# The second half of a feed-forward, with weight pairs that move on one by one

## The chip, the cores and the metric

One core of a Trainium2 chip runs the whole program. The metric is the device time of one execution in microseconds; for the kernel before it is the median of three runs. The profile is of one execution, with times counted from the first instruction.

## The reference

One layer of a hybrid encoder for 2048 tokens (16 learned ones are put in front, and dropped at the end), model width 1024, feed-forward width 2816, all float32. The change lies in the last step:

```python
f = causal_dwconv(rms_norm(h, norm_ffn_pre[l]) @ ffn_up[l], ffn_conv[l])
gate, val = jnp.split(f, 2, axis=-1)
f = (jax.nn.gelu(gate, approximate=True) * val) @ ffn_down[l]
h = h + rms_norm(f, norm_ffn_post[l])
```

The stages before it (an input projection with three groups of heads, attention among them, and an output projection) aren't touched.

## The kernel before

Matrix products in float32 are made of three passes over split operands: each operand is kept as a high and a low part (`split`: ScalarE copies the high part, then VectorE or GpSimd subtracts it from the source to get the low one), and `mm3` multiplies high by high, high by low and low by high.

The **up stage** (`ffn_up`) walks over 3 groups of tokens times 22 blocks of 128 columns, a unit each. A unit makes seven products by a scheme that saves one of eight (Strassen's in Winograd's form: sums and differences of operands go in, and sums of products come out). Its products use three PSUM banks, and two sets of three alternate between units. Then come a convolution of three taps (`conv`: one ScalarE instruction, L1723, and two on VectorE, L1725), a GELU on ScalarE, the gate times value on GpSimd (L1731), and a store to the scratch tensor `ff`. `between` runs at the start of each unit and weaves other work in: normalising the next tokens, sums of the down weights, and, in one unit of the last group, the first weights of the down stage.

The **down stage** (`Down`) multiplies `ff` by `ffn_down`. The 2816 rows are taken as ten pairs of 256 rows and a rest of 256. The tokens are taken as eight blocks of 256. A weight pair is seven operands of 128 x 512, high and low, of which four are sums that lie ready in the scratch tensor `ds`; `down_operands` loads each into a raw buffer (L1814, 256 KB) and splits it (L1594 on ScalarE, L1595 on VectorE for five and on GpSimd for two). For each visit of a token block to a weight pair, `side` loads the activations `u` (L1831), makes four sums on GpSimd (L1838 to L1841) and splits seven blocks into `fo`, of which two buffers exist. Then come seven products of three passes each.

Operand slots are 35, enough for five pairs: nine on the space of the up stage's activations (`kept`, tile name `qd`) and 26 in a ring of three pools (`dw`). So the stage runs in two halves:

```python
for pair in range(pairs):
    steps.first(pair, ks[0], weights)
...
for pair in range(pairs):
    steps.second(pair, ks[1], weights, last)
```

`first` visits each token block with pairs 0 to 4 and stores partial sums to the scratch tensor `part`. `second` visits each with pairs 5 to 9 and with the rest, adds `part` on GpSimd (L1883), and ends with `add_normed`: squares summed on ScalarE, a root, a scaling by root and gain (L1522) and an addition to the residual (L1523), and the store. Between the two halves all 35 operands are replaced.

A visit accumulates in seven PSUM banks (eight with the rest) of a pool of eight, which lies where the up stage's banks were. The order of the instructions on each engine is made ahead by a scheduler that works by program order and its own timeline; each engine then runs its queue in that order. All the loads and stores in question are issued on SyncE's queue.

## Time and profile before

| | |
|---|---|
| median of three runs | 3072.59 us (3067.38, 3072.59, 3078.05) |
| profiled execution | span 3071.8 us; its own time isn't told apart from the runs |
| mean granted TensorE clock | 0.969 |
| TensorE matmul busy | 2921.6 us (95%) |
| VectorE, ScalarE, GpSimd busy | 2054.8, 1482.3, 1358.8 us |
| up stage on TensorE | 1678.5 to 2597.2 us |
| down stage on TensorE | 2597.3 to 3060.3 us |

PE is TensorE, DVE VectorE, ACT ScalarE, POOL GpSimd, SP SyncE. A row names a line of the kernel, an engine, an operation, and the tile it writes and those it reads. In a row of a window stand the stretch, its length, and for each engine the busy time with the number of instructions, then the granted TensorE clock (1.00 is full), the mean busy share of the DMA engines, and GB/s. In a row of a wait stand who waited, what ended the wait, and the sum, the number and the longest of them in us. In a row of a tile stand the least, middle and greatest duration in ns, and the first and last start. In a timeline stand start and duration in us, and in brackets the idle time before it and who ended it. Matmuls overlap: one of 512 columns is shown with 390 ns, and the next starts 230 ns after it.

### The profile page before, as it was taken

The page shows a single profiled execution, that of the slowest core. Times are in us where ns is not written, and L with a number is a line of the kernel's source. Part 1 is how long each engine was busy: PE and PEld are TensorE (multiplying, and loading weights), DVE is VectorE, ACT ScalarE, POOL GpSimd, SP SyncE. Part 2 cuts the span into 40 slices and gives each one's busy share as a digit, 9 for nine tenths or more (in the row PEclk, how much of TensorE's full clock was granted, in tenths as well). Part 3 has the DMA queues.
Part 4 walks back from the last instruction along what each step waited for, and adds up shares of the span by engine and source line. Part 5 has one row for each costly group of instructions (what it writes and reads, how often), then busy time and mean ns, then how long its engine had stood idle before and what let it go on. Part 6 is the DMA issues. An engine that isn't in the chain of part 4 may idle for free. (4 is left out here: it accounts for less than half of the span.)

```text
span 3071.8 us, 52793 instructions
## 1 busy us (share of the span) xinstructions
PE 2921.6 (95%) x18694; PEld 2495.2 (81%) x18694; DVE 2054.8 (67%) x3934; ACT 1482.3 (48%) x2853; POOL 1358.8 (44%) x1589
## 2 busy tenths in 40 slices
PE   6999999999989999999989899999999999999998
PEld 6998898888876654665558899999999998787876
DVE  5268645656667785556635788888778786547766
ACT  4245332443336553555534656666566665324333
POOL 1001121122114555667842457445655444547765
PEclk9998999999988898999999999999999999999999
DMA  6776578466654346535245555566777765435444
GB/s 211 244 237 207 161 244 287 156 211 204 196 153 94 88 104 199 133 99 122 62 129 173 168 182 180 169 201 208 214 215 216 219 189 171 161 104 171 149 160 144
DMA packets 467818, 532.58 MB, mean 173 GB/s; under 512 B 85488, under 2 KB 355514, under 8 KB 466000
## 3 DMA queue, kind: packets, MB, share of 16 engines
q1 hardware_dynamic: 467168, 528.81, 56.5%
q8 instruction: 147, 2.41, 0.3%
q14 instruction: 119, 0.97, 0.1%
q0 software_dynamic: 384, 0.39, 0.0%
HBM read 369.11 MB, written 159.95 MB: 172 GB/s over the span
## 5 line engine op out<-in xcount | busy, mean ns | idle before, releaser
L172 PE MATMUL psu<-xo,uw 128*128 128x344 f32 x1848 | 589.9, 323 | 16.7 <-ACT xo L1594 6.9
L173 PE MATMUL psu<-xo,uw 128*128 128x344 f32 x1848 | 592.6, 321 | 0.0
L174 PE MATMUL psu<-xo,uw 128*128 128x344 f32 x1848 | 582.9, 320 | 0.0
L172 PE MATMUL psp<-xh,wh 128*128 128x384 f32 (+2 forms) x1152 | 383.6, 333 | 4.1 <-ACT wh L166 2.4
L174 PE MATMUL psp<-xh,wl 128*128 128x384 f32 (+2 forms) x1152 | 380.7, 331 | 3.5 <-DMA wl<-scr_wk 3.5
L173 PE MATMUL psp<-xl,wh 128*128 128x384 f32 (+2 forms) x1152 | 380.5, 330 | 0.0
L172 PEld LDWEIGHTS psu<-xo,uw 128*128 128x128 f32 x1848 | 346.9, 188 | 20.3 <-ACT xo L1594 7.1
L1595 DVE TENSOR_TENSOR uw<-uq,uw 128x512 fp32r<-128x512 f32 x341 | 316.2, 933 | 70.3 <-ACT uw L1594 63.7
L173 PEld LDWEIGHTS psu<-xo,uw 128*128 128x128 f32 x1848 | 347.9, 188 | 0.3 <-DVE xo L1595 0.3
L174 PEld LDWEIGHTS psu<-xo,uw 128*128 128x128 f32 x1848 | 346.5, 188 | 0.0
L1594 ACT ACTIVATE uw<-uq 128x512 fp32r<-128x512 f32 x462 | 287.9, 627 | 110.1 <-PE psu L174 48.7
L686 ACT ACTIVATE p<-sc,bias 128x512 f32<-128x512 f32 (+4 forms) x352 | 195.8, 590 | 178.5 <-PE sc L682 146.3
L1725 DVE SCALAR_TENSOR_TENSOR uy<-psu,ffn_cols,uy 128x342 f32<-128x342 f32 (+1 forms) x396 | 223.9, 567 | 60.7 <-ACT uy L1723 59.1
L559 DVE TENSOR_REDUCE mc<-mx 128x1 f32<-128x512 f32 (+6 forms) x352 | 190.3, 565 | 100.9 <-PE mx L554 75.8
L1731 POOL TENSOR_TENSOR uy<-uy,uy 128x342 f32<-128x342 f32 (+1 forms) x132 | 140.6, 1065 | 253.2 <-DVE uy L1725 77.4
L725 POOL TENSOR_TENSOR acc<-acc,p 128x512 f32<-128x512 f32 (+3 forms) x208 | 221.8, 1068 | 60.3 <-ACT p L686 23.9
L1595 POOL TENSOR_TENSOR uw<-uq,uw 128x512 fp32r<-128x512 f32 x121 | 177.9, 1470 | 125.0 <-ACT uw L1594 92.7
L174 PEld LDWEIGHTS psp<-xh,wl 128*128 128x128 f32 x1152 | 222.1, 193 | 13.0 <-issue 6.1
L172 PEld LDWEIGHTS psp<-xh,wh 128*128 128x128 f32 x1152 | 222.1, 193 | 10.7 <-issue 4.0
L173 PEld LDWEIGHTS psp<-xl,wh 128*128 128x128 f32 x1152 | 222.1, 193 | 7.6 <-issue 5.5
L1595 DVE TENSOR_TENSOR fo<-u,fo 128x896 fp32r<-128x896 f32 x88 | 112.6, 1279 | 121.3 <-ACT fo L1594 121.3
L1594 ACT ACTIVATE fo<-u 128x896 fp32r<-128x896 f32 x88 | 81.1, 922 | 206.3 <-POOL u L1841 106.8
(465 smaller groups left out, 6470.4 us busy)
## 6 DMA issues: line engine op xcount, KB each, us to landing
uq<-scr_us SPq DMA_DIRECT2D x220, 256.0 KB
uq<-in_ffn_up_dram SPq DMA_DIRECT2D x209, 256.0 KB
wl<-scr_wk SPq DMA_DIRECT2D x48, 512.0 KB
wh<-scr_wk SPq DMA_DIRECT2D x48, 512.0 KB
u<-scr_ff SPq DMA_DIRECT2D x88, 256.0 KB
scr_ff<-uy SPq DMA_DIRECT2D x110, 171.0 KB
raw<-in_w_in_dram SPq DMA_DIRECT2D x24, 512.0 KB
scr_wk<-wh SPq DMA_DIRECT2D x24, 512.0 KB
```

What stands on the lines that cost most here:

```text
L172: nc.tensor.matmul(out, ah, bh, start=first, stop=False, skip_group_check=more)
L173: nc.tensor.matmul(out, ah, bl, start=False, stop=False, skip_group_check=more)
L174: nc.tensor.matmul(out, al, bh, start=False, stop=last, skip_group_check=more)
L559: self.reduced = nc.vector.tensor_reduce(mc[:rows, i, ci : ci + 1], ps[:rows, : e - a], axis=AX.X, op=ALU.max)
L686: last = nc.scalar.activation(p[:rows, :w], ps[:rows, :w], AF.Exp, bias=bias[:rows, j : j + 1])
L725: eng.tensor_tensor(a, ps_[0][0][:rows, c0:n] if start and i == 1 else a, p[:rows, : n - c0], op=ALU.add)
L1594: core.nc.scalar.activation(hi, src, AF.Copy)
L1595: (eng or core.nc.vector).tensor_tensor(lo, src, hi, op=ALU.subtract)
L1725: stt(y[:, :n], src[:, i : n + i], cw[:, 44 * i + cc : 44 * i + cc + 1], y[:, :n], op0=ALU.mult, op1=ALU.add)
L1731: core.pooled = nc.gpsimd.tensor_tensor(v[:, :n], g[:, :n], v[:, :n], op=ALU.mult)
```

## The change

- **Moving pairs.** A visit still takes five weight pairs, but they move on: in the first half, block p starts at pair 5p // 8, so that blocks 0 to 7 start at pairs 0, 0, 1, 1, 2, 3, 3, 4. In the second half each block takes the five that it hasn't had, by the same rule starting at 5 and counted around from ten to zero. Pairs 0 to 3 are therefore prepared a second time, as 10 to 13: 14 preparations in place of 10. Slots are reused in a fixed ring of 35.
- **Four more kept slots.** The pools of the normalised tokens and their gain (`np`, `gf`) are opened outside the up stage, and their four tiles become operand slots there; the ring's second pool has four fewer. So 13 operands, not 7, are prepared during the last group of the up stage: pair 0 at unit 13 and six of pair 1 at unit 17.
- **Held splits.** The remaining splits of pairs 0 to 3 are queued behind the up stage's last convolution instruction on ScalarE and on VectorE (an order of issue on that engine alone).
- **Rest weights.** They are loaded in the seventh visit of the first half, queued behind that visit's last ScalarE copy of `la` and last store.
- **Banks read by copies.** In the last unit of the up stage the sums of products p3 and p2 are written to the tiles `u2` and `ga` rather than to their bank, and p4 is copied to a tile by ScalarE, and the convolutions read these.
- **`add_scaled`** takes the place of `add_normed` in the down stage: the gain is multiplied in before the root is ready, and the root comes in with the addition.

```diff
+def add_scaled(core, pool, halves, gain, x, junk):
+
+    nc = core.nc
+    v = pool.tile([P, 8], F32, tag="rs2", name=core.n("rs2"))
+    sums = v[:, 4:5], v[:, 5:6]
+    for y, acc in zip(halves, sums):
+        nc.scalar.activation(junk, y, AF.Square, accum_out=acc)
+    for c, y in enumerate(halves):
+        nc.vector.tensor_tensor(y, y, gain[:, 512 * c : 512 * c + 512], op=ALU.mult)
+    r1 = rstd_root(core, v, sums, D)
+    for c, y in enumerate(halves):
+        xc = x[:, 512 * c : 512 * c + 512]
+        nc.vector.scalar_tensor_tensor(xc, y, r1, xc, op0=ALU.mult, op1=ALU.add)
...
-DOWN_KEPT = 9
-
-DOWN_SLOTS = 5, 13, 8
-DOWN_TURNS = (2, 3), (0, 5), (1, 13), (2, 5)
-DOWN_FROM = 14
+DOWN_KEPT, DOWN_NORM = 9, 3
+
+DOWN_SLOTS = 5, 9, 8
+DOWN_TURNS = (2, 3), (0, 5), (1, 9), (2, 5)
+DOWN_FROM = 13, 17
+DOWN_HELD = 4
+DOWN_REST = 6
...
             elif name == "p3":
-                tt(ps, ps, u2, op=ALU.add)
-                gb = conv(ps, 0, j, n[1])
+                sum_ = ps if more else u2
+                tt(sum_, ps, u2, op=ALU.add)
+                gb = conv(sum_, 0, j, n[1])
...
             else:
-                va = conv(ps, 1, j, n[0])
+                src = ps
+                if not more:
+                    src = s("ga")
+                    nc.scalar.activation(src, ps, AF.Copy)
+                va = conv(src, 1, j, n[0])
                 ending(ga, va, j, b0[0], n[0])
...
+def down_visits(pairs):
+
+    for half in range(2):
+        for pair in range(pairs):
+            first = DOWN_CUT * pair // pairs + DOWN_CUT * half
+            yield half, pair, range(first, first + DOWN_CUT)
...
         for k in ks:
-            side, w = self.side(k, pair), weights(k)
+            side, w = self.side(k % DOWN_PAIRS, pair), weights(k)
...
-            add_normed(core, self.spool, halves, P, self.gain, hx, [junk] * 2)
+            add_scaled(core, self.spool, halves, self.gain, hx, junk)
...
+        def slot():
+            down.append(down.pop(0))
+            home = down[-1]
+            return home.tile([P, 2, 512], F32R, tag="dw", name=core.n("dw")) if hasattr(home, "tile") else home
...
                 down.extend(kept[:, i] for i in range(DOWN_KEPT))
+                for pl, tag in [(np_, "nt_x")] * DOWN_NORM + [(gf, "g_fpre")]:
+                    down.append(pl.tile([P, 2, 512], F32R, tag=tag, name=core.n("kd"))[:])
             elif sup == SUPERS:
-                if j == DOWN_FROM:
+                if j in DOWN_FROM:
                     raw = lambda: tmp.tile([P, 512], F32, tag="uq", name=core.n("raw"))[:]
-                    ws.append(down_operands(core, raw, lambda: down.pop(0), a["ffn_down"], scr, 0))
+                    k = DOWN_FROM.index(j)
+                    some = range(min(len(DOWN_PRODUCTS), len(down) - len(DOWN_PRODUCTS) * k))
+                    ws[k] = down_operands(core, raw, slot, a["ffn_down"], scr, k, some)
...
+        down[:0] = [dws[i] for i, n in DOWN_TURNS for _ in range(n)]
...
+        ended = core.taken.ins, core.conved.ins
+
+        def weights(c):
+            have = ws.setdefault(c, [])
+            if len(have) < len(DOWN_PRODUCTS):
+                raw = lambda: dwr.tile([P, 512], F32, tag="dq", name=core.n("raw"))[:]
+                with ExitStack() as behind:
+                    for ins in ended if c < DOWN_HELD else ():
+                        behind.enter_context(tc.issue_after(ins))
+                    some = range(len(have), len(DOWN_PRODUCTS))
+                    have += down_operands(core, raw, slot, a["ffn_down"], scr, c % DOWN_PAIRS, some)
+            return have
...
+        for half, pair, ks in down_visits(pairs):
+            if half == 0:
+                steps.first(pair, ks, weights)
...
+                if pair == DOWN_REST:
+                    with tc.issue_after(core.copied.ins), tc.issue_after(core.stored.ins):
+                        for i in range(2):
+                            rest.append(dwn.tile([P, 2, D], F32R, tag=f"r{i}", name=core.n("dwn")))
+                            at = P * (2 * DOWN_PAIRS + i)
+                            load_parts(core, (dpo, "hx", None), a["ffn_down"][at : at + P, :], rest[i][:, 0], rest[i][:, 1])
+            else:
+                steps.second(pair, ks, weights, last)
```

`core.taken` and `core.conved` are the up stage's last ScalarE and VectorE convolution instructions, `core.copied` and `core.stored` the down stage's last copy of `la` and last store of `part` at that point.

67 lines of the change are left out of this document (24 added, 43 removed).

## The prediction

> **What bounds the kernel now.** I read the first and second part of the page first, then the second half of the feed-forward (from about 2597 us to the end) in windows, then the waits of TensorE alone there, and the timeline around the two places where those waits lie.
>
> ```profile
> span 3071.8 us, 52793 instructions
> ...
> PE 2921.6 (95%) x18694; PEld 2495.2 (81%) x18694; DVE 2054.8 (67%) x3934; ACT 1482.3 (48%) x2853; POOL 1358.8 (44%) x1589
> ```
>
> TensorE is the bound over the whole span, so only its idle time can be won back. How many matmuls this stage has is told by the rows of its accumulator tiles, one form of three:
>
> ```profile
> L172 PE MATMUL psd<-dw,fo x416: 388/392/632, 2612.9 to 3054.4; 128*128 128x512 f32 x139
> ...
> L172 PE MATMUL psd<-qd,fo x144: 390/395/765, 2597.3 to 3035.4; 128*128 128x512 f32 x144
> ...
> L172 PE MATMUL psd<-dwn,fo x64: 388/394/394, 2841.7 to 3059.9; 128*128 128x512 f32 x64
> ...
> L174 PE MATMUL psd<-dwn,fo x64: 388/392/394, 2842.8 to 3060.3; 128*128 128x512 f32 x64
> ```
>
> 416 + 144 + 64 = 624, times three passes: 1872 matmuls. By the code these are eight visits of 5 x 7 x 3 = 105 and eight of 105 + 24 = 129. In windows of the stage (first visit; visits two to seven; the last of the first half and the first of the second; the other seven; the tail):
>
> ```profile
> core 0: us, PE busy (x) PEld busy (x) DVE busy (x) ACT busy (x) POOL busy (x), PEclk, DMA share, GB/s
> 2597.00:2637.00 40.00, 31.54 (x109) 23.68 (x108) 26.44 (x30) 22.03 (x35) 22.10 (x26) 0.79 0.66 227
> 2637.00:2782.00 145.00, 145.00 (x631) 118.41 (x631) 68.85 (x81) 38.06 (x48) 75.06 (x121) 1.00 0.32 107
> 2782.00:2847.00 65.00, 58.22 (x235) 45.52 (x235) 54.39 (x55) 32.30 (x52) 49.79 (x52) 0.95 0.56 183
> 2847.00:3061.00 214.00, 211.21 (x905) 168.59 (x903) 149.88 (x192) 72.51 (x136) 142.17 (x163) 1.00 0.47 155
> 3061.00:3071.80 10.80, 0.00 (x0) 0.00 (x0) 6.36 (x14) 2.17 (x8) 0.54 (x1) 0.66 0.41 146
> ```
>
> Visits two to seven are the undisturbed pace: 145.00 / 6 = 24.17 us, or 0.2302 us a matmul, so a visit of 129 should take 29.70. Cut at their first matmuls, the two visits of the third window are
>
> ```profile
> 2782.04:2810.66 28.62, 24.78 (x107) 19.40 (x105) 24.82 (x25) 15.91 (x26) 23.34 (x22) 1.00 0.65 211
> 2810.66:2847.17 36.51, 33.57 (x130) 26.25 (x131) 29.69 (x31) 16.39 (x27) 26.62 (x31) 0.91 0.49 161
> ```
>
> The lost time is then: first visit 39.7 (2597.3 to 2637.0) - 24.17 = 15.6; the change of halves 28.62 + 36.51 - 24.17 - 29.70 = 11.3; the last seven 214.0 - 7 x 29.70 = 6.1, or 0.87 each. In all 33.0 us, 1.1% of the span: this is the most that the stage can give. What TensorE waited for, in the first window, the third, and the fourth:
>
> ```profile
> PE psd L172 <- DVE uy L1725: 3.0, 1, 3.0
> PE psd L172 <- ACT uy L1727: 2.9, 1, 2.9
> PE psd L173 <- DVE dw L1595: 2.1, 1, 2.1
> PE psd L172 <- ACT dw L1594: 0.4, 1, 0.4
> ```
> ```profile
> PE psd L172 <- ACT fo L1594: 3.9, 2, 3.7
> PE psd L174 <- DVE fo L1595: 2.7, 2, 2.3
> ```
> ```profile
> PE psd L172 <- ACT fo L1594: 2.3, 5, 0.6
> ```
>
> So two causes, not one. At the start TensorE waits for banks that the convolution of the last up unit still reads (uy), then for weights (dw). At the change of halves it never waits for a weight: it waits for the activation operand `fo`, whose sums and splits (`side`) queue behind a burst of 35 weight operands on ScalarE, VectorE and GpSimd.
>
> **The change, part by part.** *Banks and the held splits.* The timeline of VectorE and of TensorE at the start:
>
> ```profile
> 2595.88 2.44 DVE L1595 TENSOR_TENSOR dw<-raw,dw 128x512 fp32r<-128x512 f32 x3 [0.19 <-ACT dw L1594]
> ...
> 2600.02 1.04 DVE L1725 SCALAR_TENSOR_TENSOR uy<-psu,ffn_cols,uy 128x342 f32<-128x342 f32 x2
> ...
> 2604.98 0.57 DVE L1725 SCALAR_TENSOR_TENSOR uy<-psu,ffn_cols,uy 128x342 f32<-128x342 f32 x1
> ```
> ```profile
> 2605.69 0.76 PE L172 MATMUL psd<-qd,fo 128*128 128x512 f32 x1 [2.87 <-ACT uy L1727]
> 2606.26 0.63 PE L173 MATMUL psd<-qd,fo 128*128 128x512 f32 x1
> 2606.68 0.63 PE L174 MATMUL psd<-qd,fo 128*128 128x512 f32 x1
> ```
>
> Weight splits sit between the last convolutions, the last of which ends at 2605.6, and the bank goes free only then. After the change the sums land in `u2` and `ga`, and product p4 is copied out by one ACT instruction, so the last bank is free about one copy after the last up matmul; the splits of pairs 1 to 3 on ScalarE and VectorE queue behind the last convolution, which should then end near 2600.5 instead. The copy adds one ACT instruction (nearest row 0.63 us, below) on a chain that nobody in this visit waits for. Both bank waits go: 3.0 + 2.9. With them goes most of the slow pace behind them: matmuls at 2606 take 0.63 us against a usual 0.39, and about a dozen start 0.43 apart, about 3 us in all. That is 9 of the 15.6.
>
> *What is late next: the weights.* Thirteen operands are ready instead of seven, so the visit needs 22 more. Eight fit the raw buffers and lie loaded; then the hold keeps them from being split until about 2599 (ScalarE) and 2600.5 (VectorE). The other 14 loads wait behind that in SP's queue, and with them the loads of `u`, which ScalarE and GpSimd need for `fo`. 14 + 5 transfers of 128 x 512 x 4 bytes are 5.0 MB, at the 227 GB/s of the first window 22 us: from 2600.5 to 2622.5, and the split of the last comes behind. An unbroken visit ends at 2621.5. Prices of one operand, and of one `fo` split:
>
> ```profile
> L1594 ACT ACTIVATE dw<-raw x52: 612/629/635, 2594.7 to 2828.6; 128x512 fp32r<-128x512 f32 x52
> L1595 DVE TENSOR_TENSOR dw<-raw,dw x36: 678/944/1774, 2595.9 to 2831.9; 128x512 fp32r<-128x512 f32 x36
> L1595 POOL TENSOR_TENSOR dw<-raw,dw x16: 1267/1533/1824, 2599.7 to 2828.7; 128x512 fp32r<-128x512 f32 x16
> ...
> L1595 DVE TENSOR_TENSOR fo<-u,fo x88: 691/1230/2187, 2586.7 to 3051.1; 128x896 fp32r<-128x896 f32 x80, 128x512 fp32r<-128x512 f32 x8
> ```
>
> VectorE: 16 of the 22 at 0.944 is 15.1, and four `fo` splits at 1.23 another 5: 20 us from 2600.5, to 2620.6, just in time if nothing collides. I take a loss of 5 us (3 late, 2 of slow pace) where 15.6 was; bounds 0 and 15.6.
>
> *The rest weights* (two loads of 512 KB, two splits on ScalarE and on VectorE) leave the first visit, where the first is issued at
>
> ```profile
> 2602.58 0.42 SPq L165 DMA_DIRECT2D raw<-in_ffn_down_dram  x1
> ```
>
> for the seventh, behind a copy and a store of it. This is 1 MB, some 4.6 us of transfers at that rate, off the tightest place; it is in the 5 us above. In the seventh visit I cost it at nothing: ScalarE works 38.06 of 145 us there. Without that cover it would be two operands of double size, under 4 us.
>
> *Six more operands in the up stage.* Work of this kind falls into
>
> ```profile
> 2480.00:2520.00 40.00, 40.00 (x255) 40.00 (x254) 34.01 (x55) 26.55 (x55) 18.39 (x16) 1.00 0.72 207
> 2520.00:2560.00 40.00, 40.00 (x255) 40.00 (x254) 29.91 (x49) 24.36 (x50) 13.14 (x14) 1.00 0.58 165
> ```
>
> TensorE is full in both. Six operands add at most 4 x 0.944 to VectorE, 6 x 0.629 to ScalarE, 2 x 1.533 to GpSimd: the second window would still be below the first on VectorE. Zero, hidden by that slack; the slots (`nt_x` and `g_fpre`) have been idle since the last normalisation.
>
> *The moving pairs.* The change of halves goes: a new pair's slots come free with the first fifth of one visit, and its operands are needed in the last fifth of the next, some 38 us for 7 operands. But 14 pairs are now prepared, not 10, and the bill for the change of halves tells what a pair can cost where `fo` is late: 11.3 / 5 = 2.25 us (of which the clock of 0.95 over 65 us, behind two long waits, is some 0.6). Four (5 to 8) fall into visits two to eight of the first half, where ScalarE waits for TensorE rather than the other way:
>
> ```profile
> ACT fo L1594 <- PE psd L174: 69.8, 16, 5.8
> ```
>
> That is 69.8 us in six visits, so `fo` is ready ahead, and I take 0.25 us a pair (0 to 2.25). Five (9 to 13) fall into the second half, where there is no such cushion: it loses 0.87 a visit, `fo` waits for the sums of GpSimd, and those for their load. Against the burst the density is low, one pair in some 50 us instead of one in 8, and waits under a microsecond leave the clock at 1.00 in the fourth window. I take 1.0 us a pair, nearer to the 0.87 that a whole visit loses now than to the 2.25 of the burst; bounds 0 and 2.25, and more in a rival below.
>
> *A rule against this.* Where both engines work on SBUF operands, the same split takes longer:
>
> ```profile
> 2797.30 2.18 DVE L1595 TENSOR_TENSOR fo<-u,fo 128x896 fp32r<-128x896 f32 x1
> ```
> ```profile
> 2796.80 1.74 POOL L1595 TENSOR_TENSOR qd<-raw,qd 128x512 fp32r<-128x512 f32 x1
> ```
>
> against 1.23 us in the middle for that `fo` split and 1.27 at least for that of GpSimd. The Trainium skill, SBUF — State Buffer, section "Who interferes with whom", says that a VectorE instruction with two SBUF inputs and a GpSimd one that reads SBUF exclude each other for a whole instruction. By that rule each added pair would lengthen a visit by its whole time on both engines, and the sum would be that of the second rival; the stretched rows agree with it, the fourth window only partly.
>
> *The norm at the end of a visit.* `add_scaled` has the same four long VectorE instructions for a row block as before, two of them ahead of the root. In seven visits this is beside TensorE. In the tail VectorE is the bound:
>
> ```profile
> 3065.20 0.75 DVE L1522 SCALAR_TENSOR_TENSOR lb<-lb,rs,g_fpost 128x512 f32<-128x512 f32 x1
> ...
> 3067.14 0.69 DVE L1523 TENSOR_TENSOR hx<-hx,rb 128x512 f32<-128x512 f32 x1
> ```
>
> It works 6.36 of the 6.8 us from 3061.0 until the last of these ends, so the order can win what is idle, 0.5 us; bounds 1.5 (two long instructions taken off the end) and -0.5.
>
> **The sum.** Lost time after: first visit 5.0; rest of the first half 4 x 0.25 = 1.0; second half 8 x 0.87 + 5 x 1.0 = 12.0: 18.0 against 33.0. With 0.5 of the tail the gain is 15.5. The profiled span of 3071.8 lies 0.8 under the median of the runs shown (3072.59, of 3067.38 to 3078.05), and I carry that over: 3072.6 - 15.5 = 3057.1.
>
> **The rivals.**
>
> First, every pair costs what it did in the burst, wherever it falls. 9 x 2.25 = 20.3; lost time 5.0 + 7.0 + 20.3 = 32.3, gain 0.7 + 0.5, time 3071.4: no change. For it: it is the one measured price. Against: the cushion of 69.8 us, and the clock part of that price.
>
> Second, and slower: VectorE and GpSimd become the bound of the second half. The place is `side`: GpSimd's four sums and VectorE's `fo` split stand in fixed queues behind the new splits. At the shortest rows a pair is 5 x 0.678 + 2 x 1.267 = 5.9 us of the two engines; if they can't overlap and the visit has no room, five pairs add 29.6. Lost time 5.0 + 7.0 + 29.6 = 41.6 against 33.0, less 0.5: 8.1 us slower, 3080.7. It decides from where the two engines' working time leaves no room in a visit of 29.7. For it: in the fourth window they are busy 149.88 + 142.17 = 292 us in 214, and the window before it lost 11.3 us, 3 of them by its slower clock, under a load of this kind. Against: 292 in 214 shows that they do overlap a good deal, and in visits two to seven 68.85 + 75.06 fill 143.9 of 145 us without any loss.
>
> Third, the hold takes back at the start what the banks give. ScalarE and VectorE split nothing before 2599, the raw buffers stay full, SP's queue stands, `u` is late too, TensorE waits over 3 us twice and its pace drops again; the first visit loses 15 us as before. Gain 15.5 - 10 = 5.5, time 3067.1. For it: 22 us of transfers against 21. Against: now 28 operands and the rest weights pass in the same 40 us, so 22 without them should take less.
>
> Fourth, nothing added is seen: 1 us lost in the first visit, 7.0 in the second half, no price for pairs. Lost 8.0, gain 25.5, time 3047.1.
>
> **How the numbers follow.** Forecast 0.57; first rival 0.13, second 0.12, third 0.10, fourth 0.08. The forecast's own range, from the terms 0 to 9 (first visit) and 0 to 1.8 a pair in the second half, is 3049 to 3066. The range for 8 in 10 goes on to the fourth rival's side and past the first: 3045 to 3076; it leaves out most of the second. About 0.3%, 9.2 us, is what a measurement of this kernel can tell from no change, so faster means under 3063.4: nearly all of the forecast and the fourth rival, 0.64. Within it: the first and third rival and a rest of the forecast, 0.23. Slower: the second rival and a little of the first, 0.13.
>
> **What would show it.** Right, step by step: the last convolution on VectorE ends some 3.5 us after the last up matmul, not 8.5, and TensorE's waits on `uy` are gone; the first visit is under 31 us and its clock above 0.9; no visit of the middle is longer than 32 us; the waits for `fo` in the second half grow, but single ones stay under about 1.5 us and the clock stays at 1.00; ScalarE has 28 more weight splits. Wrong: a first visit of 35 us or more (third rival); second-half visits that hold a new pair at 32 to 36 us, with VectorE near 28 of 30 busy (first and second); a weight `dw` or `qd` as the releaser of TensorE in the middle visits, which I expect nowhere after the first; or new gaps in the up stage, whose rows I took as unchanged.

## The result, and the profile after

The changed kernel takes 3089.93 us (median of eight runs, 3084.55 to 3100.59) against 3071.81 of the kernel before on the same chip (eight runs, 3065.68 to 3085.76). The ratio is 1.0059, interval 1.0043 to 1.0075: slower by 0.6%. The forecast was 3057.1, faster by 0.5%, and the range 3045 to 3076: the time moved the other way.

The head of the page of the kernel after:

```profile
span 3092.4 us, 52912 instructions
...
PE 2916.9 (94%) x18694; PEld 2493.5 (81%) x18694; DVE 2071.3 (67%) x3954; ACT 1493.1 (48%) x2882; POOL 1368.3 (44%) x1597
```

Windows of the down stage after, cut at first matmuls like those of before: the first visit; visits two to seven; the last of the first half; the whole second half; the tail.

```profile
2612.76:2639.35 26.59, 25.95 (x105) 20.74 (x106) 16.37 (x18) 12.50 (x19) 16.01 (x22) 0.94 0.62 201
2639.35:2784.79 145.44, 145.26 (x632) 118.41 (x631) 90.19 (x100) 53.81 (x76) 94.90 (x130) 1.00 0.46 150
2784.79:2810.75 25.96, 24.70 (x107) 19.59 (x106) 17.77 (x19) 11.59 (x17) 16.60 (x23) 1.00 0.67 235
2810.74:3080.39 269.65, 250.29 (x1033) 198.56 (x1031) 180.99 (x230) 93.83 (x174) 154.79 (x195) 0.96 0.47 152
3080.35:3092.40 12.05, 0.21 (x1) 0.00 (x0) 7.74 (x14) 2.65 (x8) 1.01 (x1) 0.63 0.36 131
```

The second half of before, as one row:

```profile
2810.66:3060.56 249.90, 244.44 (x1032) 194.71 (x1032) 178.96 (x222) 88.46 (x163) 168.19 (x193) 0.99 0.48 156
```

What TensorE waited for after, from the end of the up stage into the second visit, and in the second half:

```profile
PE psd L172 <- ACT fo L1611: 13.0, 2, 12.4
```
```profile
PE psd L174 <- DVE fo L1612: 9.8, 5, 2.8
PE psd L172 <- ACT fo L1611: 8.5, 5, 3.0
```

The up stage's last matmul starts at 2600.03 in the profile after and at 2597.15 in that of before; the 2.9 us between them were there before this stage. From there on the two profiles compare so (the loss is against the undisturbed 24.17 and 29.70 a visit):

| us | loss before | forecast | loss after |
|---|---|---|---|
| start gap and first visit | 0.2 + 15.6 | 5.0 | 12.7 + 2.4 |
| visits two to eight, first half | 4.4 | 1.0 | 2.2 |
| second half | 12.3 | 12.0 | 32.1 |
| tail, against before | 0 | -0.5 | +0.8 |

Together 32.5 before and 50.2 after: 17.7 us more, beside 18.1 between the medians. Only the row of visits two to eight came near its forecast. The first visit is short (26.6 instead of 39.7), its waits on `uy` are gone and the change of halves costs nearly nothing; but the start lost its gain to a new wait of 12.4 us for `fo`, and the second half lost 20 us more than before.

### The profile page after: what moved, and what is told of

Read it like the earlier page. It is cut to its first block, busy times and chain, and to the rows that moved or that the text cites. A ratio compares the mean times of both kernels' runs of the same rounds, so it can differ in the third digit from the quotient of the medians.

```text
span 3092.4 us, 52912 instructions
## 1 busy us (share of the span) xinstructions
PE 2916.9 (94%) x18694; PEld 2493.5 (81%) x18694; DVE 2071.3 (67%) x3954; ACT 1493.1 (48%) x2882; POOL 1368.3 (44%) x1597
## 4 chain that ended last, share of the span: by engine, by line
PE 37%; DVE 4%; DMA 4%; issue 2%; POOL 2%; ACT 1%; SPq 0%; DVEq 0%; POOLq 0%; ACTq 0%
PE psu L172 8%; PE psu L173 8%; PE psu L174 8%; PE psd L172 3%; PE psd L174 3%; PE psd L173 3%; DMA u<-scr_ff 2%; PE pswo L174 1%; PE pswo L172 1%; PE pswo L173 1%; DMA xt<-scr_h 1%; DVE uw L1612 1%; DVE uy L1744 0%; DVE fo L1612 0%; DMA out_dram<-hx 0%
## 5 line engine op out<-in xcount | busy, mean ns | idle before, releaser
L172 PEld LDWEIGHTS psp<-xh,wh 128*128 128x128 f32 x1152 | 221.6, 192 | 12.3 <-ACT wh L166 4.2
L1612 DVE TENSOR_TENSOR fo<-u,fo 128x896 fp32r<-128x896 f32 x88 | 101.2, 1152 | 123.5 <-ACT fo L1611 123.5
```

Source lines behind the costliest of these rows:

```text
L172: nc.tensor.matmul(out, ah, bh, start=first, stop=False, skip_group_check=more)
L1612: (eng or core.nc.vector).tensor_tensor(lo, src, hi, op=ALU.subtract)
```

## The experiments

Executions of one kernel differ by up to 20 us (those of before lie between 3065.68 and 3085.76), and in the profiles of the kernels the up stage ends anywhere between 2592 and 2612 us. So each run is read by its ratio to before and by its stage in the trace. The ratio need not equal the quotient of the medians. The table is cut from the traces, one profiled execution a kernel (start: from the start of the last up matmul to that of the first down matmul; tail: from the start of the last matmul to the end):

| kernel | ratio, interval | start | first visit | last of first half | second half | tail |
|---|---|---|---|---|---|---|
| before | | 0.16 | 39.73 | 28.61 | 249.9 | 11.25 |
| after | 1.0059 (1.0043 to 1.0075) | 12.72 | 26.60 | 25.96 | 269.6 | 12.03 |
| e1 | 1.0052 (1.0034 to 1.0071) | 0.16 | 33.29 | 26.18 | 264.6 | 12.01 |
| e2 | 1.0033 (1.0018 to 1.0049) | 12.61 | 26.84 | 33.82 | 253.8 | 12.26 |
| e3 | 0.9970 (0.9958 to 0.9982) | 12.95 | 26.81 | 25.00 | 242.6 | 12.25 |
| e4 | 0.9998 (0.9981 to 1.0014) | 0.16 | 31.90 | 32.49 | 251.5 | 12.37 |
| f9 | 1.0026 (1.0006 to 1.0045) | 10.85 | 29.31 | 33.01 | 250.6 | 12.32 |
| f5 | 1.0020 (1.0003 to 1.0038) | 12.62 | 27.07 | 25.27 | 257.5 | |
| f6 | 1.0041 (1.0026 to 1.0056) | 12.71 | 26.75 | 25.65 | 262.9 | |
| g4 | 1.0044 (1.0029 to 1.0059) | 12.75 | 26.53 | 25.84 | 260.5 | |
| f7 | 1.0030 (1.0016 to 1.0043) | 12.68 | 26.61 | 24.65 | 257.7 | 12.03 |
| g1 | 1.0043 (1.0029 to 1.0056) | 12.60 | 27.07 | 25.16 | 260.5 | |
| g2 | 1.0027 (1.0016 to 1.0038) | 0.16 | 32.12 | 24.89 | 258.8 | 11.01 |
| g3 | 0.9979 (0.9963 to 0.9995) | 0.15 | 35.00 | 25.11 | 251.5 | 11.01 |
| h1 | 0.9971 (0.9957 to 0.9985) | 0.16 | 35.47 | 25.63 | 246.3 | 11.24 |
| h2 | 0.9962 (0.9938 to 0.9986) | 0.16 | 32.52 | 25.39 | 244.2 | 11.24 |
| h3 | one run | 12.55 | 27.05 | 25.52 | 264.2 | 11.02 |

From the end of the up stage to the end of the program, trace and ratio tell the same difference from before within 6 us for all that have both, but for g2: there the trace is 2.6 us shorter than that of before, and the ratio says 8.3 us longer. No run tells why. The intervals of f6, g4 and g1 reach well into that of the changed kernel, so what their stages say in the traces is the weaker evidence.

### The start: the kept slots, and what lies on their memory

**e1_no_kept**: the four more kept slots undone; the two pools open inside the up stage again.

```diff
-DOWN_SLOTS = 5, 9, 8
-DOWN_TURNS = (2, 3), (0, 5), (1, 9), (2, 5)
-DOWN_FROM = 13, 17
+DOWN_SLOTS = 5, 13, 8
+DOWN_TURNS = (2, 3), (0, 5), (1, 13), (2, 5)
+DOWN_FROM = (14,)
...
-    np_ = pool(ctx, "np", DOWN_NORM, **early)
-    gf = pool(ctx, "gf", 1, **early)
     with ExitStack() as p3:
...
         ps_f = [pool(p3, "ps_f0", 3, space=PSUM, **early)]
+        np_ = pool(p3, "np", DOWN_NORM, **early)
         tmp = pool(p3, "tmp", RAWS, **early)
-        g_fpre = spread(gf, a["norm_ffn_pre"], "g_fpre")
+        g_fpre = spread(pool(p3, "gf", 1, **early), a["norm_ffn_pre"], "g_fpre")
...
```

> The changed kernel without the four more kept slots: the pools of the normalised tokens and their gain are inside the up stage again, the ring has 26 slots, and only pair 0 is prepared in the up stage. Theory M (memory): with these pools moved out, the buffers of u and fo came to lie on the raw buffers of the up stage, so the first loads of u are issued 16 us later and GpSimd's sums for the first fo stand behind the last up unit's products and the held splits; that is the 12.5 us in which TensorE stands before the down stage's first matmul. Then here u is loaded near 2578 us again, that wait falls under 1 us, and the first visit is a few us longer than in the changed kernel for want of six operands: about 8 us faster than the changed kernel, 3082 where that has 3090 and the kernel before 3072. Rival H (hold): the held splits themselves keep the first fo waiting; then the 12.5 us stay and the time stays at 3090. Both expect the second half as long as in the changed kernel.

The start gap goes (12.72 to 0.16), but with seven ready operands instead of 13 the first two visits take 33.29 and 29.87: together a loss of 15.0 with the gap, nearly as much as the 15.6 of the changed kernel. So the four slots, as they are laid out here, buy next to nothing, and they bring the gap. The seven operands alone don't make the second visit long: e4 and g2 have seven too, and take 24.26 and 24.35. In e1 that visit prepares the first moving pair, and TensorE waits 3.75 us there for `fo`:

```profile
2639.87 0.50 PE L172 MATMUL psd<-dw,fo 128*128 128x512 f32 x1 [3.75 <-ACT fo L1611]
```

**e2_fixed**: fixed pairs, 0 to 4 and then 5 to 9; the rest as changed.

```diff
-            first = DOWN_CUT * pair // pairs + DOWN_CUT * half
+            first = DOWN_CUT * half
```

> The changed kernel with fixed pairs: 0 to 4 for all blocks in the first half, 5 to 9 in the second, 10 preparations. Theory P (pairs in the second half): the four pairs 10 to 13 cost some 8 us each, because each is loaded and split in one burst at the start of a visit, among the norm of the visit before. Then here the second half is back at 31 us a visit (26 us less), and the change of halves costs its 11 us again instead of 2: about 3090 - 26 + 9 = 3073. Rival N (norm): the new order of the norm or the earlier rest weights slow the second half; then visits stay near 34 us, and with the change of halves back it is near 3099. The wait of 12.5 us at the start stays in both.

The gap stays (12.61), so the moving pairs have no part in it. The second half falls to 253.8, of which its first visit is 38.75. Fixed pairs lose 9.7 + 9.0 = 18.7 us at the change of halves here, more than the 11.3 of before.

**e4_both**: e1 and e2 together.

> Both undone: fixed pairs and no four more kept slots. What is left of the change are the banks read by copies, the held splits, the early rest weights and the new order of the norm. Theories M and P: the wait at the start and the pairs' price are gone, the change of halves costs 11 us; the start gains what the bank waits cost before, 5 to 9 us: about 3065, 7 under the kernel before. Rivals H and N: 3085 or more.

Ratio 0.9998: no difference from before. The first visit loses 7.7 instead of 15.6, with held splits, copied banks and rest weights that have left, but without the six more ready operands; that is the forecast's term of 5. The change of halves loses 17 instead of 11.3, which takes most of it back.

**f9_u_over_raws**: e4 with one line moved, so that, by the order in which the pools are opened, the pool of `u` and `fo` lies on the memory of the up stage's raw buffers (`tmp`), as it does in the changed kernel, but without the four more kept slots.

```diff
-        dpf = pool(p4, "dpf", 2, **early)
         dpe = pool(p4, "dpe0", 1, **early)
...
         dpo = pool(p4, "dpo", 2, **early)
+        dpf = pool(p4, "dpf", 2, **early)
```

> The kernel with both undone (fixed pairs, no more kept slots; 3068.5, first matmul of the down stage 0.16 us after the last of the up stage) with one line moved: the pool of u and fo is opened behind that of the norm's tiles, so that u lies on the raw buffers of the up stage, as in the changed kernel. Nothing else differs. Theory M: TensorE stands 8 to 12 us before the down stage's first matmul, and the time goes up by 4 to 8 us (the weights gain some of the wait): 3073 to 3077. Rival: the place in memory is harmless, and the 13 kept operands or their splits cause the wait: 3068.5 and 0.2 us.

The gap is back, 10.85 us, from this move alone; the ratio rises from 0.9998 to 1.0026, 8.6 us. TensorE's waits around the start, in f9 and then in e4:

```profile
PE psd L172 <- ACT fo L1611: 10.9, 2, 10.5
```
```profile
PE psd L172 <- ACT dw L1611: 1.7, 1, 1.7
PE psd L172 <- ACT fo L1611: 0.8, 2, 0.6
```

The timelines show how. On SyncE's queue (SPq), the first two loads of `u` in the kernel before, and then after:

```profile
2577.96 1.13 SPq L1831 DMA_DIRECT2D u<-scr_ff  x2
```
```profile
2594.18 0.93 SPq L1866 DMA_DIRECT2D u<-scr_ff  x2
```

On GpSimd, the first sum for `fo` and the last one, before:

```profile
2582.45 0.46 POOL L1838 TENSOR_TENSOR u<-u 128x128 f32<-128x128 f32 x1 [2.40 <-DMA u<-scr_ff]
...
2586.88 1.32 POOL L1841 TENSOR_TENSOR u<-u 128x128 f32<-128x128 f32 x1
```

GpSimd, ScalarE and TensorE after:

```profile
2600.55 1.01 POOL L1752 TENSOR_TENSOR uy<-uy,uy 128x338 f32<-128x338 f32 x1 [6.82 <-PE psu L174]
2602.06 1.27 POOL L1612 TENSOR_TENSOR dw<-raw,dw 128x512 fp32r<-128x512 f32 x1 [0.49 <-ACT dw L1611]
2603.29 0.72 POOL L1873 TENSOR_TENSOR u<-u 128x128 f32<-128x128 f32 x1
...
2607.83 1.71 POOL L1612 TENSOR_TENSOR dw<-raw,dw 128x512 fp32r<-128x512 f32 x1
...
2612.00 0.90 POOL L1876 TENSOR_TENSOR u<-u 128x128 f32<-128x128 f32 x1
```
```profile
2609.45 2.41 ACT L1611 ACTIVATE dw<-raw 128x512 fp32r<-128x512 f32 x4 [0.91 <-DMA raw<-scr_ds]
2611.77 0.93 ACT L1611 ACTIVATE fo<-u 128x896 fp32r<-128x896 f32 x1
```
```profile
2600.03 0.32 PE L174 MATMUL psu<-xo,uw 128*128 128x344 f32 x1
2612.76 0.79 PE L172 MATMUL psd<-qd,fo 128*128 128x512 f32 x1 [12.40 <-ACT fo L1611]
```

The loads come 16 us later, 13 of them against the end of the up stage; in f9 it is 13 against e4. In neither trace does the load itself wait: it stands behind a store of the up stage in SyncE's queue, and its place in that queue is what has moved. That order is made ahead, and f9 differs from e4 in the layout alone. In the order of GpSimd's queue the sums then stand behind a product of the up stage, whose wait of 6.82 us ends with TensorE's last up matmul, and between three weight splits. Before, they were done 9 us ahead of that matmul. Thirteen operands lay ready, and TensorE waited for the activations.

### The second half: what a moving pair costs

**e3_no_second**: moving pairs in the first half, fixed 5 to 9 in the second, so that the preparations 10 to 13 are left out.

```diff
-            first = DOWN_CUT * pair // pairs + DOWN_CUT * half
+            first = DOWN_CUT * half if half else DOWN_CUT * pair // pairs
```

> The changed kernel with moving pairs in the first half but pairs 5 to 9 for every block in the second: left out are the preparations of pairs 10 to 13, so most blocks get some pairs twice and miss others. Theory P: the second half falls to 30 to 31 us a visit, 26 us less in all, and the change of halves stays cheap: 3064. Rival N: second half unchanged, 3090.

The second half of e3:

```profile
2804.32:3046.96 242.64, 241.00 (x1033) 191.96 (x1031) 160.94 (x209) 80.27 (x145) 147.69 (x187) 1.00 0.44 148
```

242.6 instead of 269.6: the four pairs cost 27.0 us, 6.75 each, and the ratios of the two kernels lie 27 us apart too. TensorE's waits for `fo` fall from 18.3 to 1.4 us, and the clock is 1.00 again, not 0.96. The rest of the 27 is mostly slow pace: for the same matmuls TensorE is busy 241.00 us instead of 250.29. Without these pairs (which the right result needs) the kernel is 0.3% faster than before, even with its start gap.

How one such pair costs that much is seen in the second visit of the second half (2840.40 to 2879.13, 38.73 us), which prepares a pair. VectorE, SyncE's queue, GpSimd, ScalarE and TensorE after, and two windows of that visit:

```profile
2851.53 3.45 DVE L1612 TENSOR_TENSOR qd<-raw,qd 128x512 fp32r<-128x512 f32 x3
2854.91 1.34 DVE L1612 TENSOR_TENSOR fo<-u,fo 128x896 fp32r<-128x896 f32 x1
...
2866.02 1.69 DVE L1612 TENSOR_TENSOR fo<-u,fo 128x896 fp32r<-128x896 f32 x2 [6.65 <-ACT fo L1611]
```
```profile
2851.10 1.65 SPq L1849 DMA_DIRECT2D raw<-scr_ds  x2
2854.15 1.19 SPq L1849 DMA_DIRECT2D raw<-in_ffn_down_dram  x2
...
2856.38 0.38 SPq L1866 DMA_DIRECT2D u<-scr_ff  x1
```
```profile
2863.20 0.45 POOL L1873 TENSOR_TENSOR u<-u 128x128 f32<-128x128 f32 x1 [7.91 <-DMA u<-scr_ff]
```
```profile
2847.08 2.70 ACT L1611 ACTIVATE qd<-raw 128x512 fp32r<-128x512 f32 x5
...
2865.04 1.47 ACT L1611 ACTIVATE fo<-u 128x896 fp32r<-128x896 f32 x2 [8.77 <-POOL u L1876]
```
```profile
2856.30 1.89 PE L174 MATMUL psd<-dw,fo 128*128 128x512 f32 x7 [2.13 <-DVE fo L1612]
...
2866.04 0.80 PE L172 MATMUL psd<-dw,fo 128*128 128x512 f32 x1 [3.05 <-ACT fo L1611]
...
2867.07 0.63 PE L172 MATMUL psd<-dw,fo 128*128 128x512 f32 x1
2867.49 0.63 PE L173 MATMUL psd<-dw,fo 128*128 128x512 f32 x1
```
```profile
2847.00:2856.30 9.30, 6.79 (x30) 4.91 (x28) 9.30 (x12) 5.39 (x11) 8.03 (x8) 1.00 0.63 191
2856.40:2863.20 6.80, 6.60 (x28) 5.08 (x28) 2.93 (x5) 0.00 (x0) 0.00 (x0) 1.00 0.91 293
```

Read from the top: a `fo` split stands behind three weight splits in VectorE's queue, and TensorE waits 2.13 us for it. That split also frees one of the two `u` buffers, so the next load is issued only at 2856.38, and its sums start 6.8 us later. By then VectorE, ScalarE and GpSimd have stood idle for 6.65, 8.77 and 7.91 us, and TensorE waits another 3.05; behind that wait its matmuls start 0.43 us apart instead of 0.23. VectorE was full for the 9.3 us ahead (9.30 of them busy, with the norm of the visit before among the work), and then idle for 6.65: the loss comes from the order and not from a want of working time over the visit.

The weight loads that stand ahead of this load of `u` are not those of the pair that is split here. Counted in order, the splits of pair 10 start at 2845.95 on operands whose loads were issued by 2795.08. Each split frees a raw buffer, and the loads from 2848.12 to 2855.91 fill these buffers for pair 11, whose splits start at 2913.39. While `u` is under way, the DMA engines are 0.91 busy with what was issued around it.

**f5_no_loads, f6_no_low, g4_no_loads_no_low**: for pairs 10 to 13, no loads (the splits read a resident tile); or the low part made by a second ScalarE copy instead of a subtraction on VectorE or GpSimd; or both. The two switches, in one view:

```diff
+        if load:
             core.nc.sync.dma_start(t, src)
...
-        split(core, hl[:, 0], hl[:, 1], t, core.nc.gpsimd if i in DOWN_POOLED else None)
+        if low:
+            split(core, hl[:, 0], hl[:, 1], t, core.nc.gpsimd if i in DOWN_POOLED else None)
+        else:
+            for part in range(2):
+                core.nc.scalar.activation(hl[:, part], t, AF.Copy)
```

> The changed kernel (3090) with the 28 operands of pairs 10 to 13 split from a tile that is there already: left out are their 28 loads of 256 KB, so those pairs hold wrong weights; all their splits are made at the same places. The runs so far give 27 us for the four pairs in the second half (269.6 us with them, 242.6 without). Theory Q (queues): the burst of seven splits on VectorE and two of them on GpSimd stands ahead of the work for fo; the loads matter little: second half still above 262 us, time 3083 or more. Rival D (transfers): the loads of u wait behind the seven weight loads (one took 6.8 us where 3 is usual); then the second half falls to about 245 us, time near 3065.

> The changed kernel (3090) with all loads, but for pairs 10 to 13 the low part is a second copy by ScalarE instead of a subtraction on VectorE or GpSimd: left out are 20 splits on VectorE and 8 on GpSimd, ScalarE gets 28 copies more, and the low parts of these pairs are wrong. Theory Q: with nothing added on VectorE and GpSimd, the second half falls to some 246 us, time near 3066. Rival D: the loads are still there, so it stays above 262 us, 3083 or more.

> The changed kernel (3090) with both taken from pairs 10 to 13: no loads, and ScalarE copies instead of the subtractions on VectorE and GpSimd (those pairs hold wrong weights). If loads and low splits add up (12 and 7 of the 27 us), the second half has 250 us, time 3070; if each alone is enough to make fo late, taking both leaves nearly nothing: 243 to 245, time 3063. If ScalarE's own 14 copies a pair are what is left: 250 or more.

Of the 27.0 us, leaving out the loads takes 12.1 (7.8 of it is TensorE's busy time, with the clock back at 1.00), leaving out the low parts 6.7, and both together only 9.1. f5 lies between what the two theories said, f6 at the lower edge of the second, and g4 where ScalarE's own copies are what is left. So neither the transfers nor the engines that share the low parts are the cause by themselves. In g4 neither is left, only 14 copies a pair on ScalarE, and the second half still loses 17.9 us more than in e3. As f6 and g4 put seven copies a pair more on ScalarE, their 6.7 and 9.1 may be less than what the low parts cost. GpSimd, ScalarE and TensorE of g4:

```profile
2844.36 0.46 POOL L1881 TENSOR_TENSOR u<-u 128x128 f32<-128x128 f32 x1
```
```profile
2841.99 4.25 ACT L1856 ACTIVATE qd<-dwn 128x512 fp32r<-128x512 f32 x8
2846.14 0.93 ACT L1611 ACTIVATE fo<-u 128x896 fp32r<-128x896 f32 x1
```
```profile
2847.13 0.50 PE L172 MATMUL psd<-dw,fo 128*128 128x512 f32 x1 [4.01 <-ACT fo L1611]
```

The sums are done at 2844.8, and the `fo` split waits behind eight copies until 2846.14. Of TensorE's wait of 4.01 us these copies explain 1.3; the sums had been late already.

**f7_spread**: the operands of a pair from 5 on are made two a step in the visit that needs it, each queued behind that step's load, sums and splits of `fo`.

```diff
+            if n + 1 < len(ks):
+                weights(ks[-1], range(2 * n, min(2 * n + 2, len(DOWN_PRODUCTS))), core.sided)
```

> The changed kernel (3090) with the operands of each pair from 5 on made two by two, in the first four steps of the visit that needs the pair in its fifth, each two queued on ScalarE, VectorE, GpSimd and SyncE behind that step's own work for fo. The same work, without the burst. If it is the burst that costs (theories Q and D agree here), the four pairs cost 2 to 3 us each instead of 6.8: second half about 253 us, time 3073. If it is the sheer work on VectorE and GpSimd (rival W: both engines full in the second half), spreading changes little: 265 us or more, 3085.

The same work, only in another order, costs 15.0 instead of 27.0. By the ratios the order saves 8.9 us. The second half of 257.7 lies between the two expectations, 253 for the burst and 265 or more for sheer work.

**g1_u3**: the changed kernel with a third `u` buffer, paid for with two of eight raw buffers.

```diff
-        u = self.fpool.tile([P, 8, P], F32, tag="u", name=core.n("u"))
+        u = self.fpool.tile([P, 8, P], F32, tag="u", name=core.n("u"), bufs=3)
...
-DOWN_RAWS = 8
+DOWN_RAWS = 6
```

> The changed kernel (3090; second half 269.6 us) with three buffers for u instead of two, paid for by six raw buffers instead of eight. The runs so far: without the loads of pairs 10 to 13 the second half has 257.5, without their low splits 262.9, without the pairs 242.6. Theory L (latency): TensorE waits because u is loaded only two steps ahead, and that load stands behind the weight loads and behind a late fo split that frees its buffer; a third buffer hides much of it: second half 255 or less, time 3076 or less. Rival Q (queues): the splits and sums themselves are late on their engines, and an earlier u doesn't help: 265 or more, 3086. In both the 12.5 us at the start stay.

The second half is 9.1 us shorter, between what the two theories said, and the ratio 4.9 us. What that says of a pair needs a base with three buffers, for which h1 and h2 serve below.

**g2_one** and **g3_one_u3**: no kept slots, operands one a step over two visits, and the norm of before; g3 has the third `u` buffer too.

```diff
+            def beside(n):
+                if n < 3:
+                    ahead(ks[-1], 4 + n)
+                if n and v + 1 < len(visits):
+                    ahead(visits[v + 1][2][-1], n - 1)
```

> Moving pairs, no more kept slots (so u lies where it lay before), operands of pairs from 5 on made one by one, one in each of the last four steps of the visit before and the first three of the visit that needs the pair, each queued behind that step's own work; and the norm in the order of before. Theory (burst): spreading over two visits costs half of spreading over one (3.8 us a pair there): second half 249 to 252, start as in the kernel without kept slots (0.2 us of wait, two visits of 56), time 3064. Tail: with the old order of the norm 11.3 us after the last matmul, where the changed kernel has 12.0. Rival W (sheer work): second half 257 or more as when spread over one visit, 3071; and a tail of 12.0 if the order of the norm is not what lengthens it.

> The kernel of operands one by one (no more kept slots, old order of the norm) with three buffers for u and six raw buffers. Theory L: second half 246 or less, 3 to 6 us less than without the third buffer, time near 3060. Rival Q: the third buffer does nothing: the same second half within 1 us; two raw buffers fewer may cost a few us at the start in both.

Spreading over two visits is no better than over one (258.8 against 257.7); this is where the rival of sheer work had put it, so that rival may hold for what spreading leaves. With the third buffer it is 251.5, 7.3 less than in g2 but 5.5 more than I had expected, and g3 is the first version with moving pairs that is faster than before: 0.9979, under 1 in its whole interval.

**h1_before_u3** and **h2_fixed_u3**: the third `u` buffer (and six raw buffers) in the kernel before, and in e4 with the norm of before.

> The kernel before with a third u buffer, and six raw buffers in place of eight; nothing else is changed. Theory (a two-buffer chain for fo is what makes a burst of weight splits cost time): the change of halves, a burst of 35 operands, loses less than its 11.3 us, 5 to 9, and the second half loses 3 to 6 instead of 6.1; the time is 0.1 to 0.2% under before. Rival (the gain of the version that spreads the operands came from the spreading and from the moving pairs): the change of halves loses 10 to 13 as before, ratio 0.999 to 1.002. Fewer raw buffers could lengthen the first visit by 1 to 4 us in either case.

> The changed kernel without the four kept slots, with fixed pairs (0 to 4, then 5 to 9), with the third u buffer (six raw buffers) and with the norm of before. Against the version with moving pairs spread one operand a step and the same third buffer (ratio 0.9979; second half 251.5 us, last visit of the first half 25.1) it tells what the moving pairs still bring once fo has a third buffer. Theory (the moving pairs, spread, save the change of halves and give back 2.2 us a pair): here the change of halves loses 10 to 17 us, the other seven second-half visits are 29.7 to 30.3 each, and the ratio is 0.999 to 1.002. Rival (the third buffer alone brings it): the change of halves loses under 6 and the ratio is 0.995 to 0.998.

The second half of h2:

```profile
2800.01:3044.17 244.16, 239.28 (x1033) 192.94 (x1031) 177.95 (x225) 89.24 (x164) 165.71 (x192) 1.00 0.49 163
```

The buffer alone takes the kernel before to 0.9971, and h2 is at 0.9962. By intervals h1, h2 and g3 can't be told apart; in the traces h2 loses 17 us from the first visit to the tail, and g3 26. So the gain of g3 can be had from the buffer without moving pairs, and nothing shows that they add to it. In h1 the first visit became 4.3 us shorter, where I had thought that six raw buffers would lengthen it; with the held splits it became longer (g3 35.00 against 32.12 in g2, h2 32.52 against 31.90 in e4). In h1 the change of halves loses 7.4 (9.7 with the visit behind it) where 11.3 was lost, and all later visits but the last are at 29.64 instead of 30.1 to 30.8; in h2 the change loses 5.9 (7.6), and the later visits lie at 29.63 to 30.05. In the second half the buffer's main effect was thus that a visit is no longer late by itself; the burst of 35 operands got only partly cheaper. No run leaves out the pairs with three buffers; if eight visits of 29.70, 237.6, are taken as the base there, as the later visits of h1 and h2 suggest, a pair costs an estimated 5.7 us in g1 and 3.5 in g3, against 6.75 and 3.8 (f7) with two buffers and 242.6 as the base. Order takes nearly half of the price in these traces; the third buffer takes little of it.

### The norm

**h3_normed**: the changed kernel with `add_normed`.

```diff
-            add_scaled(core, self.spool, halves, self.gain, hx, junk)
+            add_normed(core, self.spool, halves, P, self.gain, hx, [junk] * 2)
```

> The changed kernel with the norm of before in the down stage; all else as in the changed kernel. Theory (the new norm lengthens the tail by about 0.8 us and is neutral inside the visits): the tail after the last matmul is 11.0 to 11.3 instead of 12.0, the second half stays at 267 to 272, time 3084 to 3100. Rival (the tail differs from run to run by itself): 11.8 to 12.4.

The tail is 11.02, as in g2 and g3 (11.24 or 11.25 in before, h1 and h2), against 12.0 to 12.4 in all kernels with `add_scaled`. VectorE and GpSimd in the tail of the changed kernel:

```profile
3080.36 1.55 DVE L1536 TENSOR_TENSOR la<-la,g_fpost 128x512 f32<-128x512 f32 x1 [0.19 <-ACT u L1534]
...
3082.43 0.68 DVE L1536 TENSOR_TENSOR ra<-ra,g_fpost 128x512 f32<-128x512 f32 x1
```
```profile
3080.09 1.27 POOL L1918 TENSOR_TENSOR rb<-rb,pt 128x512 f32<-128x512 f32 x1
```

The first multiplication by the gain takes 1.55 us instead of 0.68, beside GpSimd's last sum, which ends at 3081.36. These 0.87 us are about the whole difference of the tail. With the norm of before, VectorE has additions from a bank at that moment. This row agrees with the rule of the Trainium skill that the prediction weighed (SBUF — State Buffer, "Who interferes with whom"). The second half of h3 is 264.2, 5.4 less than after; I had expected no difference, and one profile doesn't settle whether the norm is its cause.

## Why the prediction was wrong

- **The bound and the places of loss** were read rightly: TensorE, three places, two causes. The last convolution ends on VectorE at 2603.7, 3.7 after the last up matmul (forecast 3.5); the waits on `uy` are gone; the first visit is under 31 us with a clock of 0.94, though 12.7 us of waiting ahead of it had given its weights time. (The forecast's own range should read 3047 to 3065 by its terms, not 3049 to 3066.)
- **"Zero, hidden by that slack; the slots (`nt_x` and `g_fpre`) have been idle since the last normalisation"**: this step failed first. The slots were idle, but their memory wasn't free: by the order of the pools, `u` had come to lie there. Keeping it shifted the pool of `u` and `fo` onto memory that the up stage still used, and a load some 13 us later turned 0 into a start gap of 12.7 us. The prediction counted the working time of six operands and did not ask what came to lie where. It also expected weights to be late next; with 13 operands ready it was `fo`. f9 shows the cause, with none of the four more kept slots in it. How the term of 5 us would have done without the gap, e4 tells: 7.7, with seven ready operands.
- **The change of halves goes, pairs in the first half are nearly free**: right here. Visits two to seven are at 24.16 to 24.63, although VectorE has 90.19 us of work in 145 where it had 68.85. The cushion of 69.8 us on ScalarE fits that. It isn't safe everywhere: in e1 the pair in the second visit came with a loss of 5.7 us there.
- **"I take 1.0 us a pair, ...; bounds 0 and 2.25"**: this step failed most. It is 6.75, for four pairs; the fifth, 9, was prepared ahead in the 25.96 us visit of the first half. The density was averaged over 50 us, but all splits of the pair shown come within 11 us of one visit. Single waits were said to stay under 1.5 us and the clock at 1.00; they were up to 3.0, and it was 0.96, which made up some 10 of the 27. The price of the burst, 2.25, was no upper bound: it divided one break by five pairs, but seven operands cost the visit shown 9.0 us, nearly as much as 35 cost at the change of halves (11.3). By the timeline the break is a turn of the chain of `fo`, and the number of operands in it matters little.
- **The second rival** had nearly the size, 5.9 a pair, but not the mechanism. It said that the two engines can't overlap and have no room. That is true of VectorE for 9.3 us of the visit shown, and then it was idle for 6.65; in the second half the two were busy 181 and 155 of 270 us, so they do overlap. In f7 the same splits cost 15.0 instead of 27.0, so the price isn't their working time, and that the size came near is luck. The prediction had tied this rival to the rule of the Trainium skill on exclusive access (SBUF — State Buffer, "Who interferes with whom"); the stretched rows show that it can lengthen an instruction, and no run parts its share of the 27 us.
- **The tail**: +0.8 instead of -0.5. That is worse than the gain's lower bound of -0.5; the stretched first multiplication wasn't thought of.

Shown by runs: the layout as the cause of the gap, the four pairs as the cause of the second half's loss, order as a third (ratios) to nearly half (traces) of that price. Argued from one visit's timeline: the turn of the chain by which a pair costs what it costs, and the part that the next pair's early loads have in it; no run holds back those loads alone. Open: why fixed pairs lose 17 to 19 us at the change of halves in e2 and e4 against 11.3 before (in e4 the last visit of the first half moves 288 GB/s where it moved 211, and TensorE waits 11.8 us for `fo` in the two visits instead of 6.6), whether the four slots would pay if `u` lay elsewhere, what the 3.5 us a pair consist of that are left in g3, and whether six raw buffers or three `u` buffers shortened the first visit of h1.

## What to carry to other kernels

Before a step is costed at nothing because its memory is idle, look at what the allocator puts in its old place, and at the issue time of the first load there. Where a helper's chain with two buffers passes four queues that run in order, as `fo` does here, don't price added work by its sum alone: a burst in one queue can hold the chain. Look in the timeline for the moment at which all helpers idle together, then spread the burst or give the chain one more buffer. Here that buffer, with two raw buffers fewer, took the kernel before to 0.9971 of its time, where the whole change took it to 1.0059.

## What the runs showed of the hardware

The middle visits of f9 take 23.94 us; those of before and, nearly all, of e4 take 24.17, all at a granted clock of 1.00. The only edit of f9 against e4 is where `u`, `fo` and their neighbours lie. No run tells why. So the pace that the prediction took as undisturbed isn't the least that this stage can have. The rows of f9 and of before (visits two to seven):

```profile
2637.14:2780.82 143.68, 143.68 (x632) 118.26 (x631) 70.66 (x80) 38.10 (x48) 75.87 (x123) 1.00 0.31 101
```
```profile
2637.04:2782.04 145.00, 145.00 (x631) 118.41 (x630) 68.85 (x81) 38.06 (x48) 75.04 (x121) 1.00 0.32 107
```

Prices of parts do not add: the loads' 12.1 and the low parts' 6.7 make 9.1 together. A likely reason, not shown by itself, is that what replaced the low parts filled another queue of the same chain.

In the visit shown, the matmuls behind the wait of 2.13 us start 0.23 us apart, and those behind the wait of 3.05 us 0.43 apart for the next five microseconds. In f5 the longest wait for `fo` is 2.4 us, and the clock of its second half is 1.00; in the changed kernel it is 3.0, and the clock 0.96. It isn't the longest wait alone: in g1 that is 2.4 too, and the clock 0.99.
